# z_pool and z_attn projected together as seven products of 512-blocks behind the attention, from block sums made in DRAM

## The chip, the cores and the metric

The kernel runs on one core of one Trainium2 chip. The metric is the device time of one execution in microseconds (us), as the median of several. The engines are named as in the profile: PE is TensorE (matmuls), PEld its weight loads, DVE VectorE, ACT ScalarE, POOL GpSimd, SP SyncE, which here only issues DMAs. DMAs are issued from the queues of SP, ACT and POOL, and each queue issues in order.

## What is computed

One decoder block with two token mixers, for 16 meta tokens and 1024 tokens of width 1024, in float32. The reference, cut to what matters:

```python
h = rmsnorm(x, norm_g)                                # 1040 x 1024
proj = jnp.einsum('bld,dn->bln', h, w_in)
u_pool, z_pool, q, k, v, z_attn, f_logit, g_pool, g_attn = jnp.split(proj, _split_points(), axis=-1)
y_pool = causal_multiscale_pool(u_pool, pool_w, pool_scale) * jax.nn.silu(z_pool)
log_f = jax.nn.log_sigmoid((f_logit + b_forget).astype(jnp.float32))
y_attn = forgetting_attention(q, k, v, log_f).reshape(B, L, ATTN_WIDTH) * jax.nn.silu(z_attn)
merged = (jax.nn.sigmoid(g_pool) * jnp.einsum('blc,cd->bld', y_pool, w_up_pool)
          + jax.nn.sigmoid(g_attn) * jnp.einsum('blc,cd->bld', y_attn, w_up_attn))
return x + jnp.einsum('bld,de->ble', merged, w_out)   # then a last rmsnorm, meta rows dropped
```

z_pool and z_attn are 512 columns each, q, k and v 512 (8 heads of 64), g_pool and g_attn 1024. Together z_pool and z_attn are the product of the 1024 x 1024 matrix h (tokens alone) with 1024 columns of w_in.

## The kernel before

Every float32 product is made of three passes over operands that are split in a high and a low part: high by high, low by high, high by low. `hh` and `hl` are the parts of h, transposed (channels on the partitions, `hh4` and `hl4` being two tiles of four blocks of 128 channels each); `whi` and `wlo` those of a weight chunk. A chunk is 128 columns of w_in: `w_chunk` (L153) and `split_w` load it by SP into a tile of the tag "raw" (L145; two buffers), make the high part on ACT (L150) and the low part on POOL (L152). `g_proj` (L164) then runs 48 matmuls of 512 columns for the 1024 tokens: two halves of 512 tokens, three passes, eight blocks of channels.

The stages, in us of the profiled span: to 62 the norm of x, the transposes and the projections of the first pair of heads; to 83 the forget gates; to 499 the attention; then what is left over of the filler, the projections of z_attn and the pooling products (to 563); then the up-projections (to 660); then the product with w_out, which before and after is made of seven block products, and the last norm.

The attention has 16 units: four pairs of heads (p), two heads of each (e), two halves of the queries (half). A unit makes scores on PE (L624, L625), and maxima, exponentials, and a high and a low part of them on DVE, ACT and POOL; then output products (`po`, L685). At its end `finish` adds the two halves of the sum on DVE (t, L693), and SP stores y (L694) and the sums (L699).

PE's order is the order of the code. Between a unit's steps `F.pull(ns)` puts in filler matmuls, as many as the factor PACE (2.05) and the DVE time of the step ask for: the chunks of q, k and v of the next pair, u, and the list `raws`: four chunks of z_pool ("zp"), eight of g_pool ("gp") and eight of g_attn ("ga"). `f_raw` copies each half of such a chunk from PSUM on ACT (st, L336) and stores it in DRAM by SP (L337). After the attention z_pool is loaded again by ACT's queue (`reload`, L766) and its silu taken; the chunks of z_attn are made by `f_za` (L800). `pool_mm` (L779) makes the pooling products from the chains of running sums on DVE (`pool_chain`, `pool_split`).

The other engines' queues are ordered by a scheduler. `after(a, b)` puts an instruction behind another in the order. `sums_of_w` (L572) makes block sums of w_out in DRAM during units 4 to 13, for the seven products at the end: `put` copies a block of 1 MB by SP, behind the last store of filler; `add` accumulates a block onto it by a DMA of POOL, behind the last pass of POOL over the attention's sums.

Of the kernel before, what the change touches and what calls it, by code (L numbers as in the profile page):

```python
# [15 lines left out]
NM = 16  # L16
# [16 lines left out]
PJ, PT = 3, 2  # L33
PACE = 2.05
LATENCY = 1800.0
# [19 lines left out]
def tile_hybrid_block(ctx, tc, x, meta, norm_g, w_in, b_forget, pool_w, pool_scale,  # L55
# [295 lines left out]
    class Fill:  # L351
# [3 lines left out]
        def add(self, name, g, gate=0, apart=False):  # L355
            self.must.append((name, g, gate, apart))
# [205 lines left out]
    WB = {"11": w_out[0][:512, :512], "12": w_out[0][:512, 512:], "21": w_out[0][512:, :512], "22": w_out[0][512:, 512:]}  # L562

    accs = []

    def put(dst, src):
        after(nc.sync.dma_start(dst, src), stores[-1])
# [3 lines left out]

    def sums_of_w(i):  # L572
        if i == 4:
            put(TD[1], WB["11"])
            put(TD[3], WB["12"])
        elif i == 6:
            add(TD[1], WB["12"])
        elif i == 7:
            add(TD[3], WB["22"])
        elif i == 9:  # L580
            put(TD[2], TD[3])
        elif i == 10:
            add(TD[2], WB["11"])
        elif i == 12:
            put(TD[4], TD[2])
        elif i == 13:
            add(TD[4], WB["21"])

# [145 lines left out]
    for i, u in enumerate(units):  # L734
        nxt = units[i + 1] if i + 1 < 16 else None
        F.now = i
        if nxt is not None and nxt.p != u.p:
            F.until(f"q{nxt.p}", f"k{nxt.p}")
        merged(list(nxt.a_steps()) if nxt else [], list(u.c_steps()))
        for b in range(u.nb - LAG, u.nb):  # L740
            F.pull(LATENCY)
            u.av(b)
        if i == 1:
            after(nc.scalar.activation(pwh, pw, AF.Copy), exps[-1])
            nc.gpsimd.tensor_tensor(pwl, pw, r32(pwh), op=ALU.subtract)
        if nxt is not None:
            nxt.maxes()
        u.finish()
        sums_of_w(i)
        if nxt is not None and nxt.p != u.p:  # L750
            F.until(f"v{nxt.p}")
            pair_fill(nxt.p + 1)
# [8 lines left out]
    def btile(name, dt=F32, tag="b"):  # L761
        return bp.tile([128, SEQ], dt, name=name, tag=tag, bufs=8)

    def reload(key):
        t = btile("rl")
        nc.scalar.dma_start(t, spill[key])  # L766
        return t

    def silu(z):
        after(nc.scalar.activation(z, z, AF.Silu), evacs[-1])  # L770

    cnt = [0]

    def bank():
        cnt[0] += 1
        return (pj if cnt[0] % 2 else p8).tile([128, 512], F32, name="pj")

    ypl = {}

    def pool_mm(zp, g, plh, pll):  # L780
        yh = btile("yh", F32R, "y")
        yl = btile("yl", F32R, "y")
        for c0, c1 in HALVES:
            ps = bank()
            run(g_mm3(ps, [(pwh[:, g], pwl[:, g], plh[:, c0:c1], pll[:, c0:c1])]))
            nc.vector.scalar_tensor_tensor(zp[:, c0:c1], ps, psc[:, g:g + 1], zp[:, c0:c1], op0=ALU.mult, op1=ALU.mult)
            nc.scalar.activation(yh[:, c0:c1], zp[:, c0:c1], AF.Copy)
            if g:
                pool_tt(yl[:, c0:c1], zp[:, c0:c1], r32(yh[:, c0:c1]), ALU.subtract)
            else:  # L790
                nc.vector.tensor_tensor(yl[:, c0:c1], zp[:, c0:c1], r32(yh[:, c0:c1]), op=ALU.subtract)
# [7 lines left out]
    def f_za(p):  # L799
        w = w_chunk(COL_ZA + 128 * p)  # L800
        za[p] = btile("za")
        for c0, c1 in HALVES:
            ps = yield from g_proj(w, c0, c1)
            evacs.append(nc.scalar.activation(za[p][:, c0:c1], ps, AF.Silu))

# [6 lines left out]

    def attn_gate(p):
        after(nc.vector.tensor_tensor(Y[p], Y[p], za[p], op=ALU.mult), los[-1])

    def attn_out(p):
        yh = hq.tile([128, SEQ], F32R, name="yah", tag="h")
        yl = hq.tile([128, SEQ], F32R, name="yal", tag="h")
        nc.scalar.activation(yh, Y[p], AF.Copy)
        nc.vector.tensor_tensor(yl, Y[p], r32(yh), op=ALU.subtract)  # L820
        ya.append((yh, yl))

    def pool_chain(g):
# [15 lines left out]
        nc.vector.scalar_tensor_tensor(u[:, NM:], s[:, NM:], 1.0 / win, u[:, NM:], op0=ALU.mult, op1=ALU.subtract)  # L839
        chains[g] = u, gp.tile([128, SEQ], F32R, name="plh", tag="g"), gp.tile([128, SEQ], F32R, name="pll", tag="g")  # L840

    def pool_split(g):
        u, plh, pll = chains[g]
        after(nc.scalar.activation(plh, u[:, NM:], AF.Copy), evacs[-1])
        return nc.vector.tensor_tensor(pll, u[:, NM:], r32(plh), op=ALU.subtract)

    chains = {}
    pool_chain(3)
    pool_chain(2)
    zp, za = [], {}  # L850
    for g in (3, 2, 1, 0):
        zp.append(reload(("zp", g)))
    zp.reverse()
    left = [f_za(p) for p in range(4)]

    def half_raw(g):
        for _ in range(3 * KO + 1):
            next(g)

    def pooled(g):  # L860
        pool_mm(zp[g], g, *chains[g][1:])

    G, gt, ya, muls = {}, {}, [], []

# [14 lines left out]
    def up(j, a, ws, sg_, prev=None):  # L879
# [8 lines left out]
        for c0, c1 in HALVES:  # L888
            ps = bank()
            run(g_mm3(ps, [(wh[:, k, :], wl[:, k, :], y[k][0][:, c0:c1], y[k][1][:, c0:c1])  # L890
                           for k in range(4)]))
# [6 lines left out]
    for p in range(3):  # L898
        attn_in(p)
    half_raw(left[0])  # L900
    pool_split(3)
    run(left[0])
    split2 = pool_split(2)
    silu(zp[3])
    silu(zp[2])
    fin = sm.tile([128, 384], F32, name="fin", tag="fz", bufs=1)
    lall = fin[:, :256].rearrange("p (u a j) -> p u a j", u=4, a=4)
    rall = fin[:, 256:320]
    rect = fin[:, 320:].rearrange("p (b r) -> p b r", b=2)
    for p in range(4):  # L910
        nc.sync.dma_start(lall[32 * p:32 * p + 32],
                          sums[4 * p:4 * p + 4].rearrange("u (a r) j -> r u a j", r=32))
    after(nc.vector.tensor_reduce(rall.rearrange("p (u j) -> p u j", u=4), lall.rearrange("p u a j -> p u j a"),
                                  axis=AX.X, op=ALU.add), split2)
    nc.vector.reciprocal(rall, rall)
    nc.vector.transpose(fin[:, 320:], rall)
    nc.sync.dma_start(recs.rearrange("(b p) r -> p b r", p=128), rect)
    pool_chain(1)
    half_raw(left[1])
    silu(zp[1])  # L920
    silu(zp[0])
    attn_in(3)
    attn_norm(0)
    attn_norm(1)
    run(left[1])
    pooled(3)
    pool_split(1)
    pool_chain(0)
    attn_norm(2)
    attn_norm(3)  # L930
    half_raw(left[2])
    run(left[2])
    pooled(2)
    pool_split(0)
    ws, rows_ = {}, {}
    ws[0, 0] = up_weights(0, 0)
    half_raw(left[3])
    attn_gate(0)
    attn_gate(1)
    pooled(1)  # L940
    attn_gate(2)
    pooled(0)
    run(left[3])
    HX.close()
    hq = ctx.enter_context(tc.tile_pool(name="hq", bufs=8, side="right", reuse_waits="tile"))
    rows_[0, 0] = gate_row(0, 0)
    ws[1, 0] = up_weights(1, 0)
    rows_[1, 0] = gate_row(1, 0)
    attn_gate(3)

# [4 lines left out]
    def w_load(n, h):  # L955
        W[n, h] = hq.tile([128, 2, 512], F32, name="W", tag="w")
        return nc.sync.dma_start(W[n, h], WSRC[n].rearrange("(k p) c -> p k c", p=128)[:, 2 * h:2 * h + 2])
# [10 lines left out]
    def operand(tag):  # L968
        return [[(bp if tag == "y" else hq).tile([128, 2, 512], F32R, name="op" + tag, tag=tag, bufs=8) for _ in range(2)]
                for _ in range(2)]  # L970

# [32 lines left out]
    for n, s in enumerate(steps):  # L1004
# [13 lines left out]
        if s == (7, 0):  # L1018
            opA, opB = operand("y"), operand("y")
        if a and j >= 4:  # L1020
# [67 lines left out]
    def prep(n):  # L1088
        A_, B_ = operand("yh"[n % 2]), operand("yh"[n % 2])
        sa = srcs[n]  # L1090
# [73 lines left out]
```

## Time and profile before

| | |
|---|---|
| times of three runs | 734.92, 734.59, 734.90 us |
| median | 734.9 us |
| span of the profiled execution, first to last instruction | 733.5 us |
| PE, DVE, ACT, POOL busy | 723.3, 529.0, 381.3, 301.0 us |
| mean granted TensorE clock | 0.997 |

The profiled execution is told by its span; what an execution's time has beside the span is the difference to the median, 1.4 us. A row of the timeline reads: start, length, engine, line, operation, what it writes and reads, shapes, how many, and in brackets the idle time ahead of it with what ended it. A row of the groups has the busy time, the mean ns of one, the idle time ahead of the group, and what ended it. A row of the DMA issues has the KB of each and the median us from issue to landing. A row of the windows has the length of the window, the busy time and the number of instructions of PE, PEld, DVE, ACT and POOL, then the granted clock, the busy share of the DMA engines and GB/s. A row of the waits has the us in total, how often, and the longest. A row of one line's instructions has the shortest, the median and the longest ns.

### The profile page before, as it was taken

The page shows a single profiled execution, that of the slowest core. Times are in us where ns is not written, and L with a number is a line of the kernel's source. Part 1 is how long each engine was busy: PE and PEld are TensorE (multiplying, and loading weights), DVE is VectorE, ACT ScalarE, POOL GpSimd, SP SyncE. Part 2 cuts the span into 40 slices and gives each one's busy share as a digit, 9 for nine tenths or more (in the row PEclk, how much of TensorE's full clock was granted, in tenths as well). Part 3 has the DMA queues.
Part 4 walks back from the last instruction along what each step waited for, and adds up shares of the span by engine and source line. Part 5 has one row for each costly group of instructions (what it writes and reads, how often), then busy time and mean ns, then how long its engine had stood idle before and what let it go on. Part 6 is the DMA issues. An engine that isn't in the chain of part 4 may idle for free.

```text
span 733.5 us, 10702 instructions
## 1 busy us (share of the span) xinstructions
PE 723.3 (99%) x3685; PEld 623.8 (85%) x3685; DVE 529.0 (72%) x1001; ACT 381.3 (52%) x794; POOL 301.0 (41%) x368
## 2 busy tenths in 40 slices
PE   9999999999999999999999999999999999999996
PEld 6997999988888898889988888888888888888885
DVE  5743667658779878788797688686289554887775
ACT  7653566456557645556554573462545423526445
POOL 5412335456326446336345374183347010006143
PEclk9999999999999999999999999999999999999998
DMA  9211131431252345312723246228385367661006
GB/s 305 61 29 30 29 97 38 132 97 52 67 161 63 87 103 114 110 50 58 177 85 101 82 138 150 73 76 295 95 230 191 110 203 267 229 258 62 1 0 230
DMA packets 82888, 86.89 MB, mean 118 GB/s; under 512 B 10465, under 2 KB 61665, under 8 KB 82802
## 3 DMA queue, kind: packets, MB, share of 16 engines
q1 hardware_dynamic: 78848, 77.29, 34.1%
q0 software_dynamic: 2112, 4.19, 3.7%
q10 hardware_dynamic: 1874, 4.72, 1.7%
q8 instruction: 29, 0.48, 0.3%
q14 instruction: 25, 0.20, 0.1%
HBM read 67.12 MB, written 27.46 MB: 129 GB/s over the span
## 4 chain that ended last, share of the span: by engine, by line
PE 91%; DVE 2%; issue 0%; ACT 0%; POOLq 0%; POOL 0%; ACTq 0%; DVEq 0%
PE pj L164 69%; PE pj L1044 8%; PE po L685 5%; PE ps L625 3%; PE ps L624 2%; PE pt L1044 2%; PE pj L509 1%; PE pj L294 0%; DVE S L664 0%; ACT S L633 0%; DVE m L640 0%; DVE pl L669 0%; DVE xt L194 0%; DVE o L1079 0%; DVE pt L655 0%
## 5 line engine op out<-in xcount | busy, mean ns | idle before, releaser
L152 POOL TENSOR_TENSOR wlo<-raw,whi 128x256 fp32r<-128x256 f32 x148 | 120.3, 864 | 190.9 <-ACT whi L150 82.3
L164 PE MATMUL pj<-hh,whi 128*128 128x512 f32 (+3 forms) x768 | 177.5, 360 | 0.2 <-DVE V L304 0.2
L164 PE MATMUL pj<-hl,whi 128*128 128x512 f32 (+3 forms) x768 | 175.7, 357 | 0.0
L164 PE MATMUL pj<-hh,wlo 128*128 128x512 f32 (+3 forms) x768 | 173.3, 356 | 0.3 <-POOL wlo L428 0.3
L164 PEld LDWEIGHTS pj<-hh,wlo 128*128 128x128 f32 x768 | 132.4, 188 | 17.3 <-POOL wlo L428 0.5
L164 PEld LDWEIGHTS pj<-hh,whi 128*128 128x128 f32 x768 | 132.2, 190 | 17.1 <-PE pj L294 0.4
L164 PEld LDWEIGHTS pj<-hl,whi 128*128 128x128 f32 x768 | 131.9, 189 | 16.4
L669 DVE TENSOR_TENSOR pl<-S,ph 128x512 fp32r<-128x512 f32 (+4 forms) x112 | 85.3, 778 | 16.6 <-ACT ph L668 15.9
L677 POOL TENSOR_TENSOR acc<-acc,S 128x272 f32<-128x272 f32 (+4 forms) x80 | 78.6, 983 | 9.5 <-ACT S L665 4.6
L633 ACT ACTIVATE S<-ps,negc 128x400 f32<-128x400 f32 (+2 forms) x96 | 49.2, 516 | 46.4 <-DVE S L631 39.1
L665 ACT ACTIVATE S<-S 128x512 f32<-128x512 f32 (+4 forms) x112 | 49.6, 479 | 31.5 <-DVE S L664 31.3
L150 ACT ACTIVATE whi<-raw 128x512 fp32r<-128x512 f32 x74 | 43.6, 624 | 34.8 <-PE pj L164 23.1
L668 ACT ACTIVATE ph<-S 128x512 fp32r<-128x512 f32 (+4 forms) x112 | 51.9, 479 | 9.6 <-PE po L685 8.7
L640 DVE TENSOR_TENSOR m<-m,S 128x272 f32<-128x272 f32 (+4 forms) x80 | 39.3, 492 | 20.9 <-ACT S L633 18.9
L664 DVE TENSOR_TENSOR S<-S,pt 128x512 f32<-128x512 f32 (+4 forms) x112 | 52.0, 497 | 0.9
L892 DVE TENSOR_TENSOR rl<-pj,rl 128x512 f32<-128x512 f32 x32 | 22.1, 690 | 30.9 <-PE pj L164 29.8
L685 PE MATMUL po<-pl,V 128*128 128x512 f32 (+4 forms) x112 | 37.5, 335 | 0.1
L625 PE MATMUL ps<-ql,ka 128*128 128x512 f32 (+4 forms) x112 | 37.4, 334 | 0.0
L336 ACT ACTIVATE st<-pj 128x512 f32<-128x512 f32 x40 | 23.8, 594 | 26.2 <-PE pj L164 21.2
L624 PE MATMUL ps<-qa,ka 128*128 128x512 f32 (+4 forms) x112 | 36.1, 322 | 0.8 <-ACT S L633 0.8
L1044 PE MATMUL pj<-opy 128*128 128x512 f32 (+1 forms) x168 | 36.2, 374 | 0.0
L685 PE MATMUL po<-ph,V 128*128 128x512 f32 (+4 forms) x112 | 36.1, 322 | 0.0
(190 smaller groups left out, 1089.5 us busy)
## 6 DMA issues: line engine op xcount, KB each, us to landing
raw<-in_w_in_dram SPq DMA_DIRECT2D x39, 512.0 KB, 4.0
xt<-in_x_dram SPq DMA_DIRECT2D x8, 512.0 KB, 7.3
sp_gp<-st SPq DMA_DIRECT2D x16, 256.0 KB, 2.0
td<-in_w_out_dram POOLq DMA_DIRECT2D x4, 1024.0 KB, 10.4
sp_ga<-st SPq DMA_DIRECT2D x16, 256.0 KB, 2.3
rl<-sp_gp SPq DMA_DIRECT2D x8, 512.0 KB, 5.0
rl<-sp_ga SPq DMA_DIRECT2D x8, 512.0 KB, 5.3
W<-td SPq DMA_DIRECT2D x8, 512.0 KB, 5.8
```

The source lines that it names most:

```text
L152: ins = nc.gpsimd.tensor_tensor(lo[:, k:k + 2], raw[:, k:k + 2], r32(hi[:, k:k + 2]), op=ALU.subtract)
L164: nc.tensor.matmul(ps, a, b, start=(i == 0), stop=(i == len(seq) - 1))
L624: nc.tensor.matmul(ps[:kb, c0:], ka[:, k0:k0 + kb], qa[:, q0 + c0:q0 + 512], start=True, stop=False)
L625: nc.tensor.matmul(ps[:kb, c0:], ka[:, k0:k0 + kb], ql[:, q0 + c0:q0 + 512], start=False, stop=True)
L633: nc.scalar.activation(s[:kb, f0:], ps[:kb, f0:], AF.Identity, bias=nb_)
L664: nc.vector.tensor_tensor(s[:kb, c0:], s[:kb, c0:], self.pm[:kb, c0:], op=ALU.subtract)
L665: exps.append(nc.scalar.activation(s[:kb, c0:], s[:kb, c0:], AF.Exp))
L668: nc.scalar.activation(ph[:kb, c0:], s[:kb, c0:], AF.Copy)
L669: dves.append(nc.vector.tensor_tensor(pl[:kb, c0:], s[:kb, c0:], r32(ph[:kb, c0:]), op=ALU.subtract))
L677: accs.append(nc.gpsimd.tensor_tensor(acc[:kb, c0:], acc[:kb, c0:], s[:kb, c0:], op=ALU.add))
L685: nc.tensor.matmul(self.po[:, c0:], v, r[:kb, c0:], start=(b == 0 and i == 0), stop=(b == self.nb - 1 and i == 1))
L1044: nc.tensor.matmul(ps, pick(A_, k, p)[:, i * 128:(i + 1) * 128], pick(B_, k, q)[:, c0:c1], start=start and n == 0, stop=n == 11, skip_grou ...
```

## The change

z_pool and z_attn are not made by chunks. Of the matrix product of h (2 x 2 blocks of 512) with the columns of w_in (2 x 2 blocks: z_attn and z_pool are the two columns) seven block products are made, by Winograd's form of Strassen's scheme, of 48 matmuls each (`g_prod`). They stand behind the attention, in the order 0 to 6; PSUM keeps four running sums from product to product. The pooling products and two rows of gates stand between the four quarters of product 6.

The operands are block sums. They are made in DRAM during the attention by the list `SUMS`: `put_h` and `add_h` write h blocks as the high part (SP) plus the low part (an accumulating DMA of POOL); the sums of w_in (`GS`) and of h (`HS`) are copies and accumulations. Two blocks of h are needed with the other sign: `put_neg` loads one in two tiles of the tag "raw" (SP), multiplies by -1 on ACT, and stores it (SP), at the end of unit 3 for block 21 and of unit 5 for block 12. After the attention the operands are loaded by SP and split: weights on ACT and POOL (`w_split`), h on ACT and DVE (`h_split`).

The filler loses the four chunks of z_pool, and PACE is 1.74. Pools and tags change: the parts of h free their halves apart (`hx`), `yh` and `yl` and the operands of the last stage swap between the pools `bp` and `hq`.

```diff
-PACE = 2.05
+PACE = 1.74
...
-    hh4 = [hp.tile([128, 4, HROW], F32R, name=f"hh{j}")[:, :, :L] for j in range(2)]
-    hl4 = [hp.tile([128, 4, HROW], F32R, name=f"hl{j}")[:, :, :L] for j in range(2)]
+    hx = [[hp.tile([128, 4, HROW], F32R, name=f"{n}{j}")[:, :, :L] for n in ("hh", "hl")] for j in range(2)]
+    hh4, hl4 = [list(t) for t in zip(*hx)]
...
+    def put_h(n):
+        put(rows_of(HS[n]), hblock(hh4, n))
+
+    def add_h(n):
+        add(rows_of(HS[n]), hblock(hl4, n))
+
+    def put_neg(n):
+        for k in range(2):
+            t = wp.tile([128, 2, 512], F32, name="neg", tag="raw")
+            put(t, rows_of(HS[n])[:, 2 * k:2 * k + 2])
+            after(nc.scalar.activation(t, t, AF.Copy, scale=-1.0), exps[-1])
+            nc.sync.dma_start(rows_of(HS["n" + n])[:, 2 * k:2 * k + 2], t)
+
+    SUMS = {
+        0: [(put_h, "21"), (put_h, "12")],
+        1: [(add_h, "21"), (put, GS[1], GB["11"])],
+        2: [(add_h, "12"), (put, GS[3], GB["12"])],
+        3: [(put_neg, "21"), (add, GS[1], GB["12"])],
+        4: [(put, TD[1], WB["11"]), (put, TD[3], WB["12"]), (add, GS[3], GB["22"])],
+        5: [(put_neg, "12"), (put_h, "11")],
+        6: [(add, TD[1], WB["12"]), (add_h, "11"), (put, GS[2], GS[3])],
+        7: [(add, TD[3], WB["22"]), (put_h, "22"), (put, HS["X"], HS["n21"])],
+        8: [(add_h, "22"), (add, rows_of(HS["X"]), rows_of(HS["11"]))],
+        9: [(put, TD[2], TD[3]), (put, HS["A"], HS["22"]), (add, GS[2], GB["11"])],
+        10: [(add, TD[2], WB["11"]), (add, rows_of(HS["A"]), rows_of(HS["n21"]))],
+        11: [(put, HS["B"], HS["A"]), (put, GS[4], GS[2])],
+        12: [(put, TD[4], TD[2]), (add, rows_of(HS["B"]), rows_of(HS["11"])), (add, GS[4], GB["21"])],
+        13: [(add, TD[4], WB["21"]), (put, HS["C"], HS["B"])],
+        14: [(add, rows_of(HS["C"]), rows_of(HS["n12"]))],
+    }
...
-    raws = [(n, j) for n, c in (("zp", 4), ("gp", 8), ("ga", 8)) for j in range(c)]
+    raws = [(n, j) for n, c in (("gp", 8), ("ga", 8)) for j in range(c)]
...
+    def w_split(n):
+        hi, lo = [[bp.tile([128, 2, 512], F32R, name="gw", tag="y", bufs=8) for _ in range(2)] for _ in range(2)]
+        for k in range(2):
+            nc.scalar.activation(hi[k], raw_w[n][k], AF.Copy)
+            for c in range(2):
+                pool_tt(lo[k][:, c], raw_w[n][k][:, c], r32(hi[k][:, c]), ALU.subtract)
+        op_w[n] = hi, lo
+
+    def h_split(n, neg=False):
+        hi, lo = [[hq.tile([128, 2, 512], F32R, name="gh", tag="h") for _ in range(2)] for _ in range(2)]
+        for k in range(2):
+            if neg:
+                nc.scalar.activation(hi[k], raw_h[n][k], AF.Copy, scale=-1.0)
+                nc.vector.scalar_tensor_tensor(lo[k], raw_h[n][k], -1.0, r32(hi[k]), op0=ALU.mult, op1=ALU.subtract)
...
+    def g_prod(ps, n, i, start):
+        m = 0
+        for p, q in ((0, 0), (0, 1), (1, 0)):
+            for k in range(4):
+                nc.tensor.matmul(ps, op_w[n][p][k // 2][:, k % 2, i * 128:(i + 1) * 128], op_h[n][q][k // 2][:, k % 2],
+                                 start=start and m == 0, stop=m == 11, skip_group_check=True)
+                m += 1
...
+    for i in range(4):
+        g_prod(gb_[i], 1, i, True)
+        plus_(za[i][:, T0_], gb_[i], 1.0)
+    HX.close()
+    hq = ctx.enter_context(tc.tile_pool(name="hq", bufs=8, side="right", reuse_waits="tile"))
+    h_split(2, True)
+    h_in(3)
+    w_in_(3)
+    w_split(3)
+    h_split(3)
+    for i in range(4):
+        g_prod(ga_[i], 2, i, False)
+        zp[i] = btile("zp")
+        keep(zp[i][:, T0_], ga_[i])
+    pool_chain(0)
+    attn_in(3)
+    attn_norm(0)
...
+    for i in range(4):
+        pool_mm(3 - i)
+        g_prod(ga_[i], 6, i, False)
+        silu(za[i][:, T1_], ga_[i])
+        if i < 2:
+            rows_[i, 0] = gate_row(i, 0)
```

On SP's queue, at the end of units 2 and 3 of before, where raw weight loads (L145) stand among the stores of z_pool's halves (L337), the sums (L699) and y (L694):

```order
L145 DMA raw<-in_w_in_dram 128x8x128
L337 DMA sp_zp_2098<-st 128x512 x2
L145 DMA raw<-in_w_in_dram 128x8x128
L699 DMA sums<-sr 128x16
L337 DMA sp_zp_2251<-st 128x512
L911 DMA fin<-sums 32x16x16
L694 DMA sp_y_768<-t 64x512
L337 DMA sp_zp_2251<-st 128x512
```

The same place of SP's queue after the change (neg is a tile of put_neg, hs_782 the block 21 of h, hsn_785 the same with the other sign):

```order
L337 DMA sp_gp_2204<-st 128x512
L579 DMA neg<-hs_782 128x2x512
L727 DMA sp_y_768<-t 64x512
L579 DMA neg<-hs_782 128x2x512
L884 DMA fin<-sums 32x16x16
L595 DMA hsn_785<-neg 128x2x512
L337 DMA sp_gp_2204<-st 128x512
L595 DMA hsn_785<-neg 128x2x512
L145 DMA raw<-in_w_in_dram 128x8x128
```

The next raw load stood ahead of the stores of the running chunk; now it stands behind both of them and behind all four transfers of put_neg. On PE at this place of the changed kernel (numbers are buffers; whi_2196 and wlo_2197 belong to the running chunk, whi_2347 to the one that the last row of SP loads):

```order
L718 MATMUL po_2052<-pl_2237,V_282 128x16
L164 MATMUL pj_2267<-hh0_119,whi_2196 128x512 x4
L164 MATMUL pj_2267<-hh1_121,whi_2196 128x512 x4
L164 MATMUL pj_2267<-hl0_120,whi_2196 128x512 x4
L164 MATMUL pj_2267<-hl1_122,whi_2196 128x512 x4
L164 MATMUL pj_2267<-hh0_119,wlo_2197 128x512 x2
L657 MATMUL ps_2324<-qa_859,ka_966 128x512
L658 MATMUL ps_2324<-ql_860,ka_966 128x512
L164 MATMUL pj_2267<-hh0_119,wlo_2197 128x512 x2
L164 MATMUL pj_2267<-hh1_121,wlo_2197 128x512 x4
L164 MATMUL pj_2361<-hh0_119,whi_2347 128x512 x3
```

From the unit's last output product (L718) to the first matmul with the next weights there are 26 matmuls of 512 columns. On ACT ahead of product 2 stand, after the change, the evacuations of products 0 and 1 (za, L941 and L944), two copies for the weights of product 3 (gw, L912) and the high parts of product 2's sum of h (gh, L921), with the silu of product 1's last block between them:

```order
L941 ACTIVATE za<-pt 128x512
L944 ACT_TABLE_LOAD
L944 ACTIVATE za<-za 128x512 x3
L912 ACTIVATE gw<-graw 128x1024 x2
L921 ACTIVATE gh<-hraw 128x1024
L944 ACTIVATE za<-za 128x512
L921 ACTIVATE gh<-hraw 128x1024
```

On DVE at the same place stand the additions of product 1 (L947), a chain of running sums (L862, L868), the normalisation of y (L842) and the low parts of the sum of h (L922):

```order
L947 TENSOR_TENSOR za<-pj,za 128x512
L862 TENSOR_TENSOR s_5800<-u 128x1039
L868 SCALAR_TENSOR_TENSOR u<-s_5800,u 128x1024
L947 TENSOR_TENSOR za<-pj,za 128x512 x2
L842 TENSOR_TENSOR y<-y,rc 128x1024
L947 TENSOR_TENSOR za<-pt,za 128x512
L922 SCALAR_TENSOR_TENSOR gh<-hraw,gh 128x1024
L842 TENSOR_TENSOR y<-y,rc 128x1024
L922 SCALAR_TENSOR_TENSOR gh<-hraw,gh 128x1024
```

Before the change the chunks of z_attn and the pooling products stood in this place, and nothing of h was split there.

More of the change, by code (lines that the diff above doesn't have):

```diff
@@ L854, in tile_hybrid_block @@
[L854 to L863, printed above, removed]
+    w_in_(1)
+    for p in range(3):
+        attn_in(p)
+    w_split(1)
+    h_in(2)
+    w_in_(2)
+    for i in range(4):
+        g_prod(ga_[i], 0, i, True)
+        za[i] = btile("za")
+        keep(za[i][:, T0_], ga_[i])
+    sums_in()
+    pool_chain(1)
+    w_split(2)
+    for i in range(4):
+        g_prod(gb_[i], 1, i, True)
+        plus_(za[i][:, T0_], gb_[i], 1.0)
@@ L896, in up @@
             gt[j] = sg_
[L898 to L934, printed above, removed]
     ws, rows_ = {}, {}
     ws[0, 0] = up_weights(0, 0)
[L937 to L946, printed above, removed]
-    ws[1, 0] = up_weights(1, 0)
-    rows_[1, 0] = gate_row(1, 0)
-    attn_gate(3)
+    ws[1, 0] = up_weights(1, 0)
+    for i in range(4):
+        pool_mm(3 - i)
[3 more added lines that the diff above has]
+            rows_[i, 0] = gate_row(i, 0)
     W = {}
```

172 lines of the change are left out of this document (118 added, 54 removed).

## The prediction

> **What bounds the kernel now.** I read the share of busy time first, then the chain of work that ended last, then the waits of TensorE, and after these the timeline where the change takes work away.
>
> ```profile
> PE 723.3 (99%) x3685; PEld 623.8 (85%) x3685; DVE 529.0 (72%) x1001; ACT 381.3 (52%) x794; POOL 301.0 (41%) x368
> ...
> PE 91%; DVE 2%; issue 0%; ACT 0%; POOLq 0%; POOL 0%; ACTq 0%; DVEq 0%
> ...
> PE pn L408 <- DVE car L544: 1.3, 1, 1.3
> PE ps L624 <- ACT S L633: 0.8, 2, 0.6
> ```
>
> TensorE (PE) is busy for 723.3 of the 733.5 us of the span and makes 91% of the last chain. Its two longest groups of waits come to 1.3 and 0.8 us. So every matmul that goes shortens the kernel by its full time, and every microsecond for which PE is made to wait is a microsecond of the result: there is no slack on PE in which a stall could vanish. The span of 733.5 us and the median of 734.9 differ by 1.4 us around the span; I keep that difference and do the sum from 734.9.
>
> **What goes.** z_pool and z_attn were eight chunks of 48 matmuls (384); they become seven products of 48 (336). All have 512 columns.
>
> ```profile
> 503.22 1.98 PE L164 MATMUL pj<-hh,whi 128*128 128x512 f32 x8
> 505.03 1.98 PE L164 MATMUL pj<-hl,whi 128*128 128x512 f32 x8
> ...
> 512.28 1.98 PE L164 MATMUL pj<-hh,wlo 128*128 128x512 f32 x8
> 514.10 1.98 PE L164 MATMUL pj<-hh,whi 128*128 128x512 f32 x8
> ```
>
> From 503.22 to 514.10 PE runs six such rows of eight, 48 matmuls in 10.88 us, 0.2267 us each. The other matmuls stay, so the saving is **10.9 us**, and with nothing else the time would be 724.0.
>
> **Stall A, at the first sign change (unit 3).** During the attention the next weight chunk is loaded by SP (L145) well ahead of its use; in the trace no matmul waits for one. The new put_neg takes both buffers in which raw weights land, and on SP's queue its loads and stores now stand ahead of the next raw load, behind the store of the running chunk's second half. PE has no other work between the last matmul of that chunk and the first of the next (the rows in the part on the change). So PE waits for a chain that begins when its own last matmul ends.
>
> ```profile
> L336 ACT ACTIVATE st<-pj 128x512 f32<-128x512 f32 x40 | 23.8, 594 | 26.2 <-PE pj L164 21.2
> ...
> L882 ACT ACTIVATE rl<-rl 128x1024 f32<-128x1024 f32 x16 | 16.7, 1046 | 0.0
> L150 ACT ACTIVATE whi<-raw 128x512 fp32r<-128x512 f32 x74 | 43.6, 624 | 34.8 <-PE pj L164 23.1
> ...
> raw<-in_w_in_dram SPq DMA_DIRECT2D x39, 512.0 KB, 4.0
> rl<-sp_gp SPq DMA_DIRECT2D x8, 512.0 KB, 5.0
> sp_gp<-st SPq DMA_DIRECT2D x16, 256.0 KB, 2.0
> rl<-sp_zp ACTq DMA_DIRECT2D x4, 512.0 KB, 7.0
> ...
> 298.98 0.32 SPq L911 DMA_DIRECT2D fin<-sums  x1
> 301.15 0.33 SPq L337 DMA_DIRECT2D sp_gp<-st  x1
> 301.57 0.45 SPq L694 DMA_DIRECT2D sp_y<-t  x1
> 302.41 0.38 SPq L145 DMA_DIRECT2D raw<-in_w_in_dram  x1
> ```
>
> The least it can be: copy of the chunk's half 0.59, the second copy with -1 behind it on ACT 1.05 (the 128x1024 row), issue of a store 0.33, issue of the raw load 0.38, landing 4.0, first half of the high part 0.62: **7.0 us**. Then a second branch, which I think comes last: the second neg load stands on SP behind the store of y, which waits for VectorE (DVE).
>
> ```profile
> 348.81 0.26 PE L685 MATMUL po<-pl,V 128*128 128x16 f32 x1
> ...
> 352.11 0.68 DVE L693 TENSOR_TENSOR t<-po,t 64x512 f32<-64x512 f32 x1
> ```
>
> From the unit's last output product to the end of t there are 352.11 + 0.68 - 348.81 = 3.98 us here. Then 0.45 (store of y) + 0.38 (neg load) + 5.0 (512 KB reloaded from DRAM, as the sp_gp row) + 1.05 + 0.33 + 0.38 + 4.0 + 0.62 = 16.2 us after that product. PE has 26 matmuls in that time, 5.9 us. So I take **10.3 us**. With the slower row for a reload (7.0) it is 12.3, so the ends are 7.0 and 12.3.
>
> **Stall B, the second sign change (unit 5).** The same pattern, but more PE work stands between: after the end of the last chunk 0.59 + 0.33 + 0.38 + 5.0 + 1.05 + 0.33 + about 3.5 for the store of 512 KB (an estimate, between the 2.0 us of 256 KB and the 5.0 of the reload) + 0.38 + 4.0 + 0.62 = 16.2 us, against attention products worth some 15.3 us of PE in the order. I take **0.9**, with ends at 0 and 3 (a reload of 7.0).
>
> **Stall C, ahead of product 2.** Product 2 needs the sums of h, split in a high part on ACT and a low one on DVE, into buffers that come free only when product 1 ends. On ACT two copies for product 3's weights now stand ahead of the first, and the silu of the last block between the two; on DVE a normalisation of y stands between the two low parts.
>
> ```profile
> 546.57 1.65 DVE L839 SCALAR_TENSOR_TENSOR u<-s,u 128x1024 f32<-128x1024 f32 x1
> 548.14 1.21 DVE L811 TENSOR_TENSOR y<-y,rc 128x1024 f32<-128x1024 f32 x1
> ...
> 551.73 1.76 DVE L811 TENSOR_TENSOR y<-y,rc 128x1024 f32<-128x1024 f32 x1
> ```
>
> A DVE pass over 128x1024 took 1.21 us alone and 1.65 to 1.76 beside others. The two copies wait for weight tiles whose last use is at the end of product 1; the second of them ends, by half a copy, some 0.55 us behind it, and the first high part 1.05 later, at 1.6. Then low part, normalisation, low part: 1.6 + 1.65 + 1.76 + 1.65 = 6.7. PE needs that second low part after six matmuls, 1.4 us into the product. So **5.3 us**; with 1.21 throughout it is 3.9, and with one step of a pooling chain (its u load stands late on SP) still ahead on DVE, 1.77 + 1.65 more, 8.7.
>
> **The rest.** The attention loses 192 filler matmuls (43.5 us); some 2.4 us of the filler that was left over move in. So the sixteen units go from 406 us to 365, and their DVE work stays.
>
> ```profile
> 221.35:247.08 25.73, 25.73 (x135) 22.49 (x134) 23.68 (x50) 16.32 (x36) 14.44 (x16) 1.00 0.18 51
> ...
> 270.37:298.53 28.16, 27.89 (x131) 22.93 (x130) 25.01 (x49) 15.90 (x40) 15.92 (x17) 1.00 0.47 108
> ...
> 322.51:350.26 27.75, 27.75 (x151) 25.08 (x151) 25.45 (x54) 19.46 (x43) 16.48 (x16) 1.00 0.17 44
> ...
> sum 405.96, PE 404.82 PEld 354.42 DVE 321.14 ACT 227.74 POOL 199.83; mean PE 25.30 PEld 22.15 DVE 20.07 ACT 14.23 POOL 12.49
> ```
>
> DVE goes from 321.14 of 406 to 88% on the mean; the densest unit has 25.45 us of DVE in 27.75, and 27.75 x 365/406 = 24.9. PE would wait 0.5 us in such a unit; over all sixteen it cannot exceed 8.0. Three units (the rows shown; the first two figures are length and PE, the fourth DVE) are about as dense: **1.5**, ends 0 and 8. POOL and ACT are about even in the attention: POOL issues twelve more accumulating DMAs of 1.03 us and loses 16 low parts.
>
> ```profile
> L152 POOL TENSOR_TENSOR wlo<-raw,whi 128x256 fp32r<-128x256 f32 x148 | 120.3, 864 | 190.9 <-ACT whi L150 82.3
> ...
> L570 POOL DMA_DIRECT2D td<-in_w_out_dram x4: 1003/1034/1288, 253.4 to 438.3; - x4
> ...
> 83.00:499.00 416.00, 414.86 (x2139) 364.13 (x2138) 330.23 (x694) 233.42 (x525) 202.65 (x233) 1.00 0.36 96
> ```
>
> The 12.4 us stand against 16 x 0.864 = 13.8. The sums add 26 transfers of 1 MB by the list in the diff, to traffic that fills 36% of the DMA engines there; the attention hides them, except where a load waits for one, which is A and B. Past the attention the weights of each product take POOL eight passes, 6.9 us by the same row and some 11 where the row is slow, beside products of 10.9 us; they are loaded a product ahead, so I cost them, the evacuations and the shortened reloads at nothing. If that cover fails it is 1 to 2 us at each of four products. For the way into the up-projections I take **0.5** (0 to 1).
>
> **The sum.** 734.9 - 10.9 + 10.3 + 0.9 + 5.3 + 1.5 + 0.5 = **742.5 us**.
>
> **Rivals.** *All is hidden*: 724.0. It speaks for it that before no chunk was waited for; for it to hold SP would have to issue the raw load before put_neg's, which its order excludes, and ACT would have to split h before product 3's weights. *Only the least of each stall*: 724.0 + 7.0 + 3.9 = 734.9, no change; it needs the second neg load to land in 1.7 us in place of 5.0, which no row of 512 KB here shows. *DVE becomes the bound of the attention*: all sixteen units at 0.5 make 8.0 in place of 1.5, 749.0. It speaks against it that the mean is 88%, and for it that the filler no longer covers the gaps. *The array runs slow after each stall*:
>
> ```profile
> 10.82 2.08 PE L164 MATMUL pj<-hh,whi 128*128 128x256 f32 x8
> 12.70 1.25 PE L164 MATMUL pj<-hl,whi 128*128 128x256 f32 x8
> ...
> 728.00:733.50 5.50, 0.00 (x0) 0.00 (x0) 0.75 (x1) 1.09 (x2) 0.64 (x2) 0.66 0.52 191
> ```
>
> Early in the span eight matmuls of 256 columns took 2.08 us, and the next eight 1.25; and in the last 5.5 us, with PE idle, the granted clock falls to 0.66. So an idle PE loses its clock, and gets it back only some time after it works again. At the price of that first row (0.8 us) to that of the first eight matmuls of the span (5.86 us instead of 1.81, that is 4.0), stalls A and C add 1.6 to 8; I take 2.0 for each, 746.5.
>
> ```profile
> 1.32 2.08 PE L408 MATMUL pn<-onesr 128*128 128x512 f32 x4 [1.32 <-DVE car L544]
> 3.33 3.78 PE L412 MATMUL gb<-grow,onesr 1*128 1x512 f32 x4
> ```
>
> The Trainium skill, "TensorE: Matmul & The Clock Gate", Part 1, has it that the default state of the array is throttled, and that an idle window of about 3.4 us sends it back to half rate until about 3.4 us of work have passed. The trace agrees as far as an idle end and a slow start show it; by that rule each long stall would cost some 1.7 us more, an estimate, and the sum would be 745.9. It speaks against this change, since before had no such stall at all.
>
> **How the numbers follow.** The forecast, with its own ends: 0.53 (738 to 746). All hidden: 0.04. The least of each: 0.11, half of it within 0.2% of 734.9 (733.4 to 736.4, about what a measurement of this kernel can tell from no change), half above. DVE as bound: 0.11. Slow clock: 0.21. Faster 0.04, same 0.06, slower 0.90. The range leaves out the hidden case, the lower half of the least one and the upper end of the last two: 736 to 751.
>
> **What would show it.** PE waits on the high part of weights (whi) of some 10 us near 170 us in the span, and behind it a raw load issued late on SP; a short one in unit 5; a wait on the low part of h ahead of product 2, 4 to 6 us; in the attention, units in which DVE is above 95%. Slow rows of eight right behind a stall speak for the clock. The prediction is wrong if SP's raw load is issued ahead of the neg stores, or if other waits after the attention come to more than a few us.

## The result, and the profile after

The changed kernel took 793.6 us (median of 793.09 to 794.09) against 734.85 before: a ratio of 1.0798, 95% interval 1.0783 to 1.0813. That is 58.8 us slower; the prediction said 742.5, with a range that ended at 751.

The lines of the page that answer to those of before, busy time, granted clock, DMA share, and the chain that ended last:

```profile
PE 730.7 (92%) x3637; PEld 620.7 (78%) x3637; DVE 554.0 (70%) x1023; ACT 398.3 (50%) x814; POOL 340.2 (43%) x404
...
PEclk9999999999599979999999999999799999999999
DMA  9111127918910794847928877289740536764005
...
PE 68%; DMA 9%; DVE 8%; ACT 5%; issue 3%; POOL 1%; SPq 0%; POOLq 0%; DVEq 0%; ACTq 0%
```

PE made 48 instructions fewer (3637, was 3685), as the change says. But it is idle for 60.7 of the 791.4 us of the span (10.2 of 733.5 before), and its busy time rose by 7.4 us where 10.9 should have gone. The chain, 91% PE before, is 68% PE now and runs through DMAs (9%), DVE (8%) and ACT (5%). The clock row has three dips (5, 7, 7). The waits of PE, and the issues of the DMAs concerned (KB, median us to landing):

```profile
PE pj L164 <- ACT whi L150: 28.7, 2, 17.2
PE ps L657 <- ACT S L666: 7.3, 8, 2.6
PE pj L932 <- ACT gh L921: 6.1, 2, 5.7
PE po L718 <- DVE pl L702: 3.4, 6, 1.0
PE pj L164 <- DVE V L304: 3.0, 2, 2.8
PE pj L932 <- DVE gh L922: 1.4, 1, 1.4
```

```profile
raw<-in_w_in_dram SPq DMA_DIRECT2D x31, 512.0 KB, 6.2
...
neg<-hs SPq DMA_DIRECT2D x4, 512.0 KB, 4.6
hsn<-neg SPq DMA_DIRECT2D x4, 512.0 KB, 9.7
```

The two waits for the high part of weights (17.2 and 11.6 us) stand at the two sign changes, the third pair (gh) ahead of product 2: stalls A, B and C are at the places in the order that the prediction named (A at 192 us, where it said about 170), and A and B are far longer. A load of raw weights that took 4.0 us before takes 6.2 on the median, and a store of put_neg 9.7. This is stall A on PE, the queue of SP, and ACT:

```profile
190.53 1.54 PE L164 MATMUL pj<-hh,wlo 128*128 128x512 f32 x6
209.23 1.65 PE L164 MATMUL pj<-hh,whi 128*128 128x512 f32 x3 [17.16 <-ACT whi L150]
```

```profile
193.86 0.36 SPq L595 DMA_DIRECT2D hsn<-neg  x1
194.34 0.40 SPq L337 DMA_DIRECT2D sp_gp<-st  x1
196.65 0.36 SPq L595 DMA_DIRECT2D hsn<-neg  x1
197.38 1.04 SPq L145 DMA_DIRECT2D raw<-in_w_in_dram  x1
```

```profile
208.55 1.15 ACT L150 ACTIVATE whi<-raw 128x512 fp32r<-128x512 f32 x2 [11.93 <-DMA raw<-in_w_in_dram]
```

The raw load is issued at 197.4 to 198.4, some 6 us after PE's last matmul ended, as the order says; but it lands only at 208.5, 10 us later. The windows around it (length, PE, PEld, DVE, ACT, POOL, granted clock, DMA share, GB/s):

```profile
192.00:198.00 6.00, 0.07 (x1) 0.00 (x0) 1.78 (x3) 3.37 (x6) 2.74 (x4) 0.74 0.91 244
198.00:209.00 11.00, 0.00 (x0) 0.00 (x0) 0.00 (x0) 0.45 (x1) 0.00 (x0) 0.50 1.07 259
209.00:215.00 6.00, 5.77 (x14) 4.51 (x15) 0.59 (x1) 3.01 (x6) 4.44 (x7) 0.50 1.05 314
```

The DMA engines are full (1.07), and the granted clock stays at 0.50 for six more microseconds after PE works again.

### The profile page after: what moved, and what is told of

Its sections match the earlier page's. It is cut to its first block, busy times and chain, and to the rows that moved or that the text cites. A ratio compares the mean times of both kernels' runs of the same rounds, so it can differ in the third digit from the quotient of the medians.

```text
span 791.4 us, 10759 instructions
## 1 busy us (share of the span) xinstructions
PE 730.7 (92%) x3637; PEld 620.7 (78%) x3637; DVE 554.0 (70%) x1023; ACT 398.3 (50%) x814; POOL 340.2 (43%) x404
## 4 chain that ended last, share of the span: by engine, by line
PE 68%; DMA 9%; DVE 8%; ACT 5%; issue 3%; POOL 1%; SPq 0%; POOLq 0%; DVEq 0%; ACTq 0%
PE pj L164 41%; PE pj L1148 8%; PE pj L932 7%; PE po L718 3%; DMA raw<-in_w_in_dram 3%; PE pt L932 2%; PE pt L1148 2%; DMA hsn<-neg 2%; PE ps L657 2%; PE ps L658 2%; ACT S L666 1%; DVE pl L702 1%; DVE m L673 1%; DMA rc<-recs 1%; DMA sp_u<-st 1%
## 5 line engine op out<-in xcount | busy, mean ns | idle before, releaser
L164 PE MATMUL pj<-hh,whi 128*128 128x512 f32 (+3 forms) x640 | 149.1, 360 | 31.8 <-ACT whi L150 28.7
L164 PEld LDWEIGHTS pj<-hh,whi 128*128 128x128 f32 x640 | 110.2, 192 | 45.2 <-ACT whi L150 29.6
L164 PE MATMUL pj<-hl,whi 128*128 128x512 f32 (+3 forms) x640 | 145.5, 354 | 0.0
L152 POOL TENSOR_TENSOR wlo<-raw,whi 128x256 fp32r<-128x256 f32 x116 | 92.7, 886 | 119.3 <-ACT whi L150 61.7
L164 PE MATMUL pj<-hh,wlo 128*128 128x512 f32 (+3 forms) x640 | 143.0, 350 | 0.0
L164 PEld LDWEIGHTS pj<-hl,whi 128*128 128x128 f32 x640 | 109.8, 191 | 12.1
L164 PEld LDWEIGHTS pj<-hh,wlo 128*128 128x128 f32 x640 | 108.4, 188 | 11.9
L136 POOL TENSOR_TENSOR gw<-graw,gw 128x256 fp32r<-128x256 f32 x48 | 50.6, 1089 | 39.6 <-ACT gw L912 17.2
L673 DVE TENSOR_TENSOR m<-m,S 128x272 f32<-128x272 f32 (+4 forms) x80 | 48.0, 601 | 26.8 <-ACT S L666 25.3
L932 PE MATMUL pj<-gh,gw 128*128 128x512 f32 x180 | 45.8, 411 | 7.5 <-ACT gh L921 6.1
L932 PEld LDWEIGHTS pj<-gh,gw 128*128 128x128 f32 x180 | 35.6, 200 | 16.8 <-ACT gh L921 7.3
L718 PE MATMUL po<-pl,V 128*128 128x512 f32 (+4 forms) x112 | 38.7, 345 | 3.6 <-DVE pl L702 3.4
## 6 DMA issues: line engine op xcount, KB each, us to landing
hs<-hl POOLq DMA_DIRECT2D x4, 1024.0 KB, 10.5
td<-in_w_out_dram POOLq DMA_DIRECT2D x4, 1024.0 KB, 10.9
```

The lines of the kernel that those rows point to most:

```text
L152: ins = nc.gpsimd.tensor_tensor(lo[:, k:k + 2], raw[:, k:k + 2], r32(hi[:, k:k + 2]), op=ALU.subtract)
L164: nc.tensor.matmul(ps, a, b, start=(i == 0), stop=(i == len(seq) - 1))
L673: nc.vector.tensor_tensor(m[:kb, c0:], m[:kb, c0:], s[:kb, c0:], op=ALU.max)
L718: nc.tensor.matmul(self.po[:, c0:], v, r[:kb, c0:], start=(b == 0 and i == 0), stop=(b == self.nb - 1 and i == 1))
L932: nc.tensor.matmul(ps, op_w[n][p][k // 2][:, k % 2, i * 128:(i + 1) * 128], op_h[n][q][k // 2][:, k % 2], start=start and m == 0, stop=m = ...
```

## The experiments

Each run is timed against the kernel before on the same chip.

**e1: put_neg in tiles of its own**

```diff
-            t = wp.tile([128, 2, 512], F32, name="neg", tag="raw")
+            t = gp.tile([128, 2, 512], F32, name="neg", tag="g")
```

> The changed kernel with one edit: put_neg's two tiles come from the pool gp (tag g) and no longer from the two buffers for raw weights. Theory (place in the queue and buffers): the raw loads are issued a chunk ahead again, both waits on whi (17.2 and 11.6 us) go, with them about 5 us of slow matmuls behind them, so 793.6 - 33 = 760 us, within 5. Rival (the DMA engines alone are too full there, wherever the load stands): waits on whi of 5 us or more stay near both places, 775 to 785 us.

767.5 us (1.0434, 1.0409 to 1.046): 26.1 us back. PE waits for whi nowhere any more, so the borrowed buffers, and with them the place of the raw loads in the queue, made both stalls. Of the 7 us by which this is short of the 33 expected, 5.4 are other waits that grew: those for S went from 7.3 to 10.5 us, those for V from 3.0 to 5.2.

**e2: product 2's sum of h first on ACT and DVE**

```diff
-    h_split(2, True)
+    ca, cv = h_split(2, True)      # the last instruction on ACT and on DVE
+    silu(za[3][:, T0_], za[3][:, T0_])
+    after(evacs[-1], ca)
...
-    w_split(3)
+    w_split(3, ca)
...
-    pool_chain(0)
+    pool_chain(0, cv)
...
-    attn_norm(0)
+    attn_norm(0, cv)
```

> The changed kernel with another order ahead of product 2 only: on ACT the two high parts of h come ahead of product 3's weights and of the last silu, on DVE the two low parts ahead of the chain of running sums 0 and of the normalisation of y. Theory (the order on ACT and DVE makes the third stall): the 7.5 us of waits ahead of product 2 and some 4 us of slow matmuls behind them shrink to 2 to 4 in all, 784 to 787 us. Rival (late loads of u and of the reciprocals or the freeing of the parts of h make it): the wait stays above 5 us, 791 to 794 us.

784.8 us (1.0674, 1.0658 to 1.069): 8.8 us back, and the 7.5 us of waits ahead of product 2 are down to 1.2. The order on the two engines made stall C.

**e3: both edits**

> Both edits together. If the two causes are independent the gains add: 760 - 8 = 752 us, within 5. What is left above 724.0 then is the attention's own lateness, not the stalls.

759.6 us (1.0332, 1.0315 to 1.0349). The gains add up, 25.3 us for the first edit and 8.0 for the second, but it ends 7.6 us above what was expected, 35.6 above 724.0. PE's longest waits are now:

```profile
PE ps L657 <- ACT S L666: 9.8, 11, 2.7
PE pj L164 <- DVE V L304: 5.3, 3, 2.9
PE po L718 <- DVE pl L702: 3.3, 6, 1.0
```

All of them are waits for the attention's own exponentials, values of v and low parts.

**e4: the block sums alone, in the kernel before.** The list SUMS and put_neg are added to it, and nothing else.

> The kernel before, with the whole list of block sums (and put_neg in the raw buffers) added during its attention and nothing else; its products don't read them. Theory (the sums, not the seven products, cost the time): waits on whi of 10 us or more near units 3 and 5 as in the changed kernel, slow matmuls behind them, and a few us of lateness elsewhere, 765 to 780 us. Rival (it takes the thinner filler and the smaller PACE to bring the stalls about; before's filler hides the sums): 735 to 742 us.

782.2 us (1.0639, 1.0623 to 1.0654), above the expected 765 to 780. Without any of the seven products, with before's filler and PACE, the two waits for whi are there, 15.9 and 20.8 us:

```profile
PE pj L164 <- ACT whi L150: 36.7, 2, 20.8
PE ps L654 <- ACT S L663: 3.5, 5, 1.1
```

**e5: no block sums, with both edits.** All entries of the list but those of w_out go; the products read other blocks that lie in DRAM, and the result isn't the reference's.

```diff
...
-        3: [(put_neg, "21"), (add, GS[1], GB["12"])],
-        4: [(put, TD[1], WB["11"]), (put, TD[3], WB["12"]), (add, GS[3], GB["22"])],
...
+        4: [(put, TD[1], WB["11"]), (put, TD[3], WB["12"])],
...
-    HSRC = [None, None, HS["B"], HS["A"], HS["C"], HS["X"], HS["22"]]
+    HSRC = [None, None, WB["11"], WB["12"], WB["21"], WB["22"], WB["11"]]
```

> The kernel with both edits (759.6 us), and the block sums of h and of w_in left out of the attention: the products read blocks of w_in and w_out that lie in DRAM anyway, so what they compute isn't the reference's; matmuls, filler, PACE and all loads after the attention stay. It tells what the 35 us above 724 are. Theory (thinner filler: DVE's work of the attention stands in 41 us less of PE work): most of it stays, 745 to 755 us. Rival (the transfers of the sums, their issue on POOL and the copies with -1 on ACT): 727 to 735 us.

744.8 us (1.0126, 1.0109 to 1.0142): 14.8 us less than with the sums, and still 20.8 above 724.0. Both theories have a part. Even if the sums cost nothing, this form of the change is slower than before.

**e6: both edits, PACE as before (2.05)**

> The kernel with both edits, PACE 2.05 as before the change and not 1.74: early units get more filler, the last ones none. Theory (thinner filler): waits move from the early units to the last ones, 752 to 768 us. Rival (the sums): the waits stay where they are, within 3 us of 759.6.

775.0 us (1.0538, 1.0523 to 1.0554), worse than either theory said. The waits did move to the end: when the filler has run out PE waits 8.1 us for one high part of the exponentials, and 7.6 us ahead of product 2:

```profile
PE po L718 <- ACT ph L701: 8.1, 1, 8.1
PE pj L937 <- ACT gh L925: 7.6, 1, 7.6
```

**e7: both edits, product 0's weights split one unit later (`i == 15` for `i == 14`)**

> The kernel with both edits, and the split of product 0's weights one unit later (unit 15 in place of 14), since near 455 us ACT stands for 5.5 us at the copy for their load, PE then 2.7 us for ACT, and the clock falls behind it. Both theories: that wait and its slow matmuls go, 753 to 756 us.

758.8 us (1.0323, 1.0307 to 1.0338): a miss. The wait of 2.7 us went, and one of 5.2 us came inside product 0, for ACT's copy of a filler half (st).

**e8: as e4, put_neg in tiles of its own**

> The kernel before with the block sums added (782.2 us with put_neg in the raw buffers), put_neg's tiles now from gp: its filler is not thinned. Theory (thinner filler makes the rest): with the two stalls gone the thicker filler hides the sums, 736 to 742 us. Rival (the sums themselves): 745 to 760 us.

745.9 us (1.0153, 1.0136 to 1.017): 36.3 us back of the 47 that the sums had cost. The 11 that stay speak for the rival: also with the full filler the sums cost something, and they cost 14.8 with the thin one.

**e9: the thin filler alone.** The kernel before; the chunks of z_pool move behind the attention:

```diff
-PACE = 2.05
+PACE = 1.74
...
-    raws = [(n, j) for n, c in (("zp", 4), ("gp", 8), ("ga", 8)) for j in range(c)]
+    raws = [(n, j) for n, c in (("gp", 8), ("ga", 8)) for j in range(c)]
...
-        zp.append(reload(("zp", g)))
+        run(f_zp(g))
```

`f_zp` is `f_za` with the columns of z_pool.

> The kernel before, with its four chunks of z_pool taken out of the filler and made behind the attention like those of z_attn, and PACE 1.74 as in the change: the same matmuls as before, no block sums, no seven products. Theory (a thinner filler alone makes PE wait for the attention's other engines; 744.8 against 724.0 without sums): 748 to 757 us. Rival (those 20 us come from the seven products' own loads, splits and orders behind the attention): 734 to 738 us.

750.8 us (1.022, 1.0205 to 1.0236): 16.2 us slower with the same matmuls; the stores and reloads of z_pool go, which is less work for the queues. The loss is in the attention. Its windows and those of the rest, before and in this run (the fields as above):

```profile
83.00:498.50 415.50, 414.36 (x2137) 363.71 (x2136) 329.76 (x693) 232.95 (x524) 202.65 (x233) 1.00 0.36 95
498.50:733.50 235.00, 228.26 (x1017) 189.19 (x1017) 156.68 (x208) 102.31 (x172) 69.73 (x85) 0.99 0.49 166
```

```profile
83.00:472.70 389.70, 379.39 (x1955) 330.44 (x1954) 331.97 (x692) 220.54 (x509) 192.54 (x217) 1.00 0.34 89
472.70:748.60 275.90, 269.41 (x1199) 223.26 (x1198) 157.11 (x208) 108.02 (x184) 79.19 (x101) 1.00 0.44 144
```

182 matmuls moved behind the attention, 41.3 us at 0.2267. The stage behind it grew by 40.9, so nothing was lost there; the attention shrank by only 25.8, and PE's idle time in it rose from 1.1 to 10.3 us. Two stretches of before, and two of this run, show how:

```profile
270.00:280.00 10.00, 10.00 (x48) 8.35 (x47) 9.74 (x17) 6.88 (x16) 7.63 (x7) 1.00 0.26 69
239.00:249.00 10.00, 10.00 (x51) 8.45 (x50) 9.18 (x24) 3.88 (x10) 2.83 (x4) 1.00 0.35 107
```

```profile
221.00:231.00 10.00, 7.98 (x36) 5.87 (x35) 9.17 (x21) 6.80 (x19) 7.48 (x9) 1.00 0.02 4
260.00:269.00 9.00, 6.99 (x48) 6.53 (x46) 8.88 (x17) 6.32 (x14) 5.55 (x4) 1.00 0.08 17
```

DVE is busy for 97 and 92% of such a stretch before too, but PE had filler to fill it with. With less (DVE 92 and 99%), PE is idle for 2 us in each. The mean over a unit does not show these stretches. That DVE sets the pace in them is read from these rows; no run made DVE's work shorter. The waits that the profile names come to 12.3 us in this run and 3.3 before. The other 6 of the span's 15.1 lie in PE's busy time, 729.3 us in place of 723.3 for the same matmuls: some 1.7 of them in a stretch at half clock (269.5 to 272.9 us), the rest not explained.

**e10: the changed kernel, the other sums moved away from put_neg**, which stays in the raw buffers:

```diff
...
-        3: [(put_neg, "21"), (add, GS[1], GB["12"])],
-        4: [(put, TD[1], WB["11"]), (put, TD[3], WB["12"]), (add, GS[3], GB["22"])],
-        5: [(put_neg, "12"), (put_h, "11")],
...
+        3: [(put_neg, "21")],
+        5: [(put_neg, "12")],
+        6: [(put_h, "11"), (put, TD[1], WB["11"]), (put, TD[3], WB["12"])],
...
```

> The changed kernel (793.6 us), put_neg still in the raw buffers, but the other block sums moved away from it: units 3 and 5 hold put_neg alone, unit 4 nothing, the rest stands one to three units earlier or later. Theory (the two stalls were longer than worked out, 17.2 and 11.6 us against 10.3 and 0.9, since other sums filled the DMA engines while the loads and stores ran): the waits come down to 10 to 12 and 1 to 5 us, 778 to 784 us. Rival (put_neg's own four transfers fill the engines, or the row of the queue is all): the waits stay within 2 us, 790 to 794 us.

784.8 us (1.0689, 1.0667 to 1.0711), just above the expected 778 to 784. Stall A is down to 10.5 us and B to 0.5. Stall A's raw load, issued at 196.5, lets ACT begin at 201.5, 5.0 us later and not 11 (197.4 to 208.5 above), and put_neg's stores land in 2.9 us and no longer in 9.7:

```profile
PE ps L656 <- ACT S L665: 12.4, 9, 6.0
PE pj L164 <- ACT whi L150: 11.0, 2, 10.5
```

```profile
raw<-in_w_in_dram SPq DMA_DIRECT2D x31, 512.0 KB, 4.7
...
hsn<-neg SPq DMA_DIRECT2D x4, 512.0 KB, 2.9
```

But of the 17.7 us by which those two waits shrank only 8.8 are left. The sums that were moved made a new wait of 6.0 us later on: ACT stood 6.5 us at a copy of a filler half (st), until the store of an earlier half had landed.

**e11: no sign change, with both edits.** put_neg is left out, and the sums take the plain blocks.

> The kernel with both edits (759.6 us), put_neg left out, the sums take the blocks with their plain sign, so the result isn't the reference's. It shares out the 14.8 us that the sums cost there (759.6 - 744.8). Theory (traffic and POOL's issues, over all units): put_neg is 2 to 4 us of them, 755 to 758 us. Rival (the copies with -1 on ACT, ahead of the exponentials, are most of it): 747 to 751 us.

755.6 us (1.0285, 1.027 to 1.03): put_neg is 3.9 of the 14.8 us; the rest is the other sums.

**e12: both edits, and the sums spread as in e10**

> The kernel with both edits and the sums spread as in the run before last. If what is left of the sums' cost comes from their bunching in units 3 to 6, 752 to 757 us; if it is spread over the attention anyway, 758 to 761 us. It stays above the kernel before in either case, since the thinner filler alone costs more than the 10.9 us saved.

766.7 us (1.0431, 1.04 to 1.0461), 7 us slower than without the spreading: a miss. Once put_neg stands in nobody's way, the spreading only brings the new wait, here of 6.4 us, on the store of a filler half. ACT shows what it stood for:

```profile
303.61 0.60 ACT L336 ACTIVATE st<-pj 128x512 f32<-128x512 f32 x1 [6.80 <-DMA sp_gp<-st]
304.10 1.26 ACT L665 ACTIVATE S<-ps,negc 128x512 f32<-128x512 f32 x2
```

## Why the prediction was wrong

The runs share the time out like this:

| step | predicted | measured | from |
|---|---|---|---|
| 48 matmuls less | -10.9 | -10.9 | the same count and rate; not measured by itself |
| stalls A and B | +11.2 | +25.3 | e2 less e3 |
| stall C | +5.3 | +8.8 | changed kernel less e2 |
| thinner filler | +1.5 | +16.2 | e9 less before |
| other cost of the sums | 0 | +14.8 | e3 less e5 |
| rest | +0.5 | +4.7 | e5 less the sum of before, -10.9 and +16.2 |

The measured column comes to 58.9, against 58.8; it adds up by construction, since the last row is what is left. The order in which edits are undone shifts it by a microsecond: taken off the changed kernel alone, A and B give 26.1; C taken off behind them gives 8.0.

- **Stall A: mechanism and chain right, size wrong.** 10.3 us were worked out, 17.2 came, and 10.5 where the other sums were moved away (e10). The chain was summed with landing times from a trace whose DMA engines were 36% busy in the attention; at this place they were full. The 4.0 us for the raw load were 10, which is most of the 6.9 us by which A came out too long.
- **Stall B: the same.** 0.9 against 11.6, and 0.5 in e10. The store of 512 KB, taken at 3.5 us, took 9.7, and the raw load behind it 9.0 in place of 4.0.
- **The sentence that the attention hides the transfers of the sums** is the first step that failed. It counted them at nothing but for A and B, with the mean share of the DMA engines. They cost 14.8 us beside the stalls, and A and B came out 14.1 us dearer than the sum had them, the slow clock behind them included. They come in bursts, and in A, B, e10 and e12 a burst reached PE through a buffer that waited for a landing: raw weights in A and B, the store of a filler half in e10 and e12. For the 14.8 that way is not shown (see what stays open). The list was also counted a little low: beside those of w_out it holds 24 transfers of 1 MB and eight of 512 KB for put_neg, and the prediction counted 26 of 1 MB.
- **The 1.5 us for DVE in the thinner attention are the second.** 1.5 us were taken, with an end at 8.0 that "cannot" be exceeded. That end compared the DVE time of a whole unit with its length. The need for filler is local: where DVE is busy for over 90% of some ten microseconds, PE needs filler there and then. e9 shows 16.2 us for the thin filler alone. "DVE becomes the bound" was a rival at 749.0; it was right, and twice as large. Neither of the two signs that were to show the prediction wrong came: SP's raw load stood behind the neg stores, and after the attention stall C alone was added. They watched neither of the two terms that failed.
- **Stall C was right within its ends** (3.9 to 8.7), but by another path. PE waited 7.5 us. Of these 6.1 (5.7 and 0.4) were for the high parts on ACT, of which the prediction had the first ready 1.6 us behind product 1; only 1.4 were for a low part on DVE, which the prediction had as the end of the chain. DVE stood 3.9 us for u's load; so product 1's additions were late, the silu on ACT behind them, and behind the silu the two copies of weights and the high part. DVE stood 1.7 us more for the reciprocals.
- **The slow clock came.** After A, B and C the rows show it, here C's:

```profile
554.50 1.22 PE L932 MATMUL pj<-gh,gw 128*128 128x512 f32 x2 [5.69 <-ACT gh L921]
556.15 2.08 PE L932 MATMUL pj<-gh,gw 128*128 128x512 f32 x4 [0.43 <-ACT gh L921]
```

Four matmuls of 512 columns take 2.08 us, as the first four of before's span did, where four a few rows earlier took 1.07. After A the clock was at 0.50 for the six microseconds of work in the window shown, so half of them, 3 us, went for it; by the same reading 1.7 us after B and 3.6 after C. The rival's 2.0 for each of A and C was of the right size, if low. Its upper end was not well founded: the second of its two rows holds matmuls of another form (1.06 us each), and no row shows what they take at full clock.

In all, PE worked some 23.5 us at half clock behind its waits in the changed kernel, so about 11.8 us of its busy time went there; that is most of the 18.3 us between the 7.4 by which the busy time rose and the 10.9 by which it should have fallen. The shares of A, B and C above hold this loss, since undoing a stall undoes its slow stretch.

The Trainium skill, "TensorE: Matmul & The Clock Gate", Part 1, has half rate after an idle window of about 3.4 us until about 3.4 us of work have passed, in windows that run on whatever the kernel does. The half rate agrees, and six microseconds fit the rest of the window in which work began again and one whole window behind it (an estimate from the page's figure).

- **What stays open.** The rest of 4.7 us was not taken apart; e5's profile still has 1.2 us of waits ahead of product 2, and the split of product 0's weights is added to ACT and POOL in the attention. Nor was it settled which of the sums, put_neg aside, make the other 10.9 of the 14.8 us. The traces of e5 and e3 show in what form the 14.8 come: the attention is 14.6 us longer (390.7 and 405.3), PE's idle time in it rises from 11.8 to 19.0, and 12.9 us of its work run at half clock, none in e5, which is 6.4 us. So nearly half is the clock that falls after the waits. No kernel here beats the one before: with the thin filler at 16.2 us against the 10.9 us saved, free sums and no stalls would not do it. A version whose products stand in the attention as filler was not tried.

## What to carry to other kernels

A chain of loads and stores that a wait will hang on is to be summed with the landing times of the traffic that will be there, not with those of a trace in which the DMA engines were about a third full. Matmuls that fill the gaps of another engine are worth more than their own time: before taking them out, look at stretches of some ten microseconds in which the other engine is busy for over 90%, not at the mean. And a small job that borrows the buffers and the queue of a prefetch takes the prefetch away; give it its own tiles, or count the whole latency.

## What was not expected of the hardware

A wait of less than three microseconds was enough to lower the clock. In the changed kernel PE waited 2.78 us at 392 to 395 us, and then ran at the lower clock for 3.4:

```profile
394.96 2.22 PE L164 MATMUL pj<-hh,whi 128*128 128x512 f32 x7 [2.78 <-DVE V L304]
```

```profile
395.00:396.00 1.00, 1.00 (x5) 0.82 (x6) 1.00 (x3) 1.00 (x3) 0.64 (x1) 1.00 0.78 184
396.00:398.00 2.00, 2.00 (x7) 1.59 (x6) 2.00 (x5) 2.00 (x7) 2.00 (x3) 0.57 0.27 75
398.00:400.00 2.00, 2.00 (x7) 1.59 (x6) 1.90 (x4) 2.00 (x5) 1.92 (x3) 0.58 0.00 0
400.00:402.00 2.00, 2.00 (x11) 1.60 (x10) 2.00 (x4) 0.19 (x1) 1.92 (x2) 1.00 0.00 0
```

The drop comes a microsecond after PE has started again, so a short wait in a dense kernel can cost more than its length, here 1.7 us more. In the changed kernel the stretches at half clock that the windows show, beside the two ends of the span, last 3.4, 3.4, 10.2, 10.2 and 20.5 us: one, three and six times 3.4. Where a wait falls decides too: the same wait of 2.2 us for V lowered the clock in e9 (269.5 to 272.9 us) and neither in e3 nor in e5.

That wait of 2.78 us begins with something that the prediction put at nothing. POOL issues an accumulating DMA and goes on without a gap to the low parts of a weight chunk; beside this run of POOL one pass of DVE takes 3.25 us (it is the first of the two in the row below), and from there DVE is busy without a break until the V that PE waits for. The rows of POOL and DVE in the changed kernel, then DVE's same two passes in e5, where POOL issues no such DMA at this place:

```profile
382.72 1.31 POOL L582 DMA_DIRECT2D hsA<-hsn  x1 [1.81 <-PE po L718]
383.51 3.33 POOL L152 TENSOR_TENSOR wlo<-raw,whi 128x256 fp32r<-128x256 f32 x4
383.76 3.46 DVE L673 TENSOR_TENSOR m<-m,S 128x144 f32<-128x144 f32 x2
```

```profile
352.32 0.52 DVE L665 TENSOR_TENSOR m<-m,S 128x144 f32<-128x144 f32 x2 [0.20 <-ACT S L658]
```

Every pass of DVE of more than 2.2 us in the attention lies beside such a run: three in before and three in e5 (2.5 to 4.1 us each, with four accumulating DMAs), eight in e3 (2.5 to 4.0 us, with sixteen). The prediction counted these DMAs on POOL alone. All this is read from the order of the rows: no run took these DMAs out by themselves, and what they cost PE in all was not measured.
